# Experts' rows added to their tokens on chip instead of in memory: an encoder block with expert-choice routing, Trainium2

## The chip, the cores and the metric

The kernel runs on one core of a Trainium2 chip. The metric is the device time of one execution in microseconds (us); the figure for the kernel before is the median of three runs. Beside it stands one profiled execution, which the hardware profiler recorded on the chip, and all rows below are from that execution.

## What is computed

A sequence of 512 tokens with 16 learned meta tokens ahead of it (528 rows of 1024 numbers, float32) goes through one layer: attention and a short convolution read one input projection, their outputs are projected back and added to the rows; then comes a mixture of experts, and a last normalisation. Each of 16 experts picks the 66 tokens with the highest affinity:

```python
logits = einsum('ld,de->le', hs, w_router);  aff = softmax(logits)
g, idx = top_k(aff.T, cap)                    # 16 experts x 66 tokens
xg = hs[idx]
a = einsum('ecd,edf->ecf', xg, w_gate);  u = einsum('ecd,edf->ecf', xg, w_up)
y = einsum('ecf,efd->ecd', silu(a) * u, w_down) * g[..., None]
out = zeros((L, D)).at[idx.reshape(-1)].add(y.reshape(-1, D))
h = h + out;   result = rms_norm(h, final_norm_g)[:, 16:, :]
```

Per expert, w_gate and w_up are 1024 x 2048 and w_down is 2048 x 1024: 24 MB of float32, 384 MB for all sixteen, each read once.

## The kernel before

**Up to the routing.** Lines 105 to 905 compute attention, convolution, the projection back (`res_pe`, `res_sum`, lines 794 to 811), the router's affinities and each expert's 66 tokens. The rows after the first half of the layer lie as five tiles of 112 tokens in `h2`. They are written to memory twice: as they are to `acc_d` (lines 845 to 848), and normalised to `hn2_d` (lines 856 to 862). `gather(e)` (line 907) then reads an expert's 66 normalised rows from `hn2_d` with an indirect DMA that POOL issues.

**Weights.** They come as tiles `raw` of 1 MB, one DMA each, into a ring of 22 buffers (`RING = (6, 6, 3, 7)`, line 38). `tasks` (lines 737 to 743) is the order of the tiles: for each expert sixteen of gate and up, and behind every second one a tile of the previous expert's down. `pump(n)` (line 746) issues DMAs on SP's queue until n tiles are under way or waiting; `nextw` (line 947) pumps and hands the next tile to PE. An issue waits until the buffer that it fills has been read.

**The stage of the experts** (lines 998 to 1029) is written in the order in which each engine runs it (`manual_schedule`). For expert e, PE multiplies each gate or up tile by the expert's gathered rows `X` (`prod`, line 951: two column tiles of 64, moving 66 columns, into banks G and U). ACT turns G into silu in `H`, VectorE (DVE) multiplies U into it. Behind every second tile, PE does one `down_piece` of expert e-1 (line 973): `H` is the stationary operand, 22 tokens at a time padded to 32 columns, and a half row of w_down of 512 columns the moving one. Four column tiles run side by side, three groups of tokens one after the other: 12 products, three banks `y`. Two of the four column tiles hold the left half of the outputs and two the right half, each for one half of the contraction.

**down_rows** (line 981) adds the two halves of the contraction and applies the gate, group by group (ACT L986, DVE L987), and POOL adds the 64 half rows of a group to `acc_d` in memory with an indirect DMA that accumulates (L988): three of those for each of the experts 0 to 14.

**The end** (lines 1051 to 1123). The last expert's down is computed transposed (L954 into `bk`), turned (L1076), and added to its tokens by products with a one-hot matrix `oh` (`by_token`, line 1046; L1049). The accumulated rows come back from `acc_d` (L1068), `add` (L1091) joins both, and each row is normalised and stored.

Of the kernel before, what the change touches and what calls it, by code (L numbers as in the profile page):

```python
# [10 lines left out]
F32 = mybir.dt.float32  # L11
# [8 lines left out]
P = 128  # L20
# [17 lines left out]
RING = (6, 6, 3, 7)  # L38
PADS = 10
# [12 lines left out]
def block_kernel(ctx: ExitStack, tc: tile.TileContext, x, meta, mix_g, w_in, conv_w, lq1, lk1, lq2,  # L52
# [708 lines left out]
    xgp = ctx.enter_context(tc.tile_pool(name="xgp", bufs=1, reuse_waits="tile"))  # L761
    rt_p = ctx.enter_context(ExitStack())
    hp = rt_p.enter_context(tc.tile_pool(name="hp", bufs=1, reuse_waits="tile"))
    h2 = hp.tile([P, NT, D], F32, name="h2")
# [7 lines left out]
    jg = hp.tile([P, 3, 2, 22], I32, name="jg")  # L772
    nc.gpsimd.iota(jg, pattern=[[-22, 3], [0, 2], [-1, 22]], base=0, channel_multiplier=1)
    sel = hp.tile([P, 3, 2, 32], F32, name="sel")
    nc.gpsimd.memset(sel, 0.0)
    nc.vector.tensor_scalar(sel[:, :, :, :22], jg, 0.0, None, op0=ALU.is_equal)

    jr = hp.tile([P, 3], I32, name="jr")
    nc.gpsimd.iota(jr[0:32, 0:1], pattern=[[0, 1]], base=0, channel_multiplier=1)
    nc.gpsimd.iota(jr[32:64, 0:1], pattern=[[0, 1]], base=0, channel_multiplier=1)  # L780
    place = hp.tile([P, 3], F32, name="place")
    nc.vector.tensor_scalar(place[:64, 0:1], jr[:64, 0:1], 21.5, None, op0=ALU.is_gt)
    nc.vector.tensor_scalar(place[:64, 1:2], jr[:64, 0:1], 2.0, 2.0 * (L - 22), op0=ALU.mult, op1=ALU.add)
    nc.vector.tensor_tensor(place[:64, 2:3], place[:64, 0:1], place[:64, 1:2], op=ALU.mult)
    nc.vector.tensor_scalar(place[32:64, 2:3], place[32:64, 2:3], 1.0, None, op0=ALU.add)
# [6 lines left out]
    lgt = lg[:TW, :NT * NE].rearrange("p (t e) -> p t e", e=NE)  # L792

    def res_pe(c):

        hT = hT_c[c]
        for t in range(NT):
            nc.tensor.matmul(lgt[:, t], hT[:, T0[t]:T0[t] + TW], wr[:, c], start=c == 0 and t == 0,
                             stop=c == DC - 1 and t == NT - 1)
        pt = tr()  # L800
        for t in range(NT):
            nc.tensor.transpose(pt[:TW, t * P:(t + 1) * P], hT[:, T0[t]:T0[t] + TW], ident)
        nc.scalar.copy(h2[:TW, :, c * P:(c + 1) * P], pt.rearrange("p (t k) -> p t k", k=P)[:TW, :NT])
# [28 lines left out]
    for t in range(NT):  # L832
        for n, a in enumerate(sq_c):
            nc.tensor.matmul(pss[:TW, t:t + 1], a[:, T0[t]:T0[t] + TW], ones[:, 0:1], start=n == 0, stop=n == 1)
    r2 = hp.tile([P, NT], F32, name="r2")
    rsqrt(r2[:TW], pss[:TW, :NT], D)
# [16 lines left out]
    nc.vector.reduce_sum(mx[:TW], af[:TW], axis=AX.X)  # L853
    nc.vector.reciprocal(mx[:TW], mx[:TW])
    nc.vector.tensor_tensor(af[:TW], af[:TW], mx[:TW, :, None].to_broadcast([TW, NT, NE]), op=ALU.mult)
# [85 lines left out]
    for h_ in HS:  # L941
        nc.gpsimd.memset(h_, 0.0)
# [210 lines left out]
```

## Time and profile before

| | us |
|---|---|
| median of three runs (1397.96 to 1399.46) | 1398.5 |
| the profiled execution, own time | 1400.15 |
| its span, from the first to the last instruction | 1398.4 |
| first product of an expert's weights | 350.9 |
| last store issued | 1392.1 |

Busy shares of the span are PE 86%, DVE 22%, ACT 15%, POOL 16%. A matmul in float32 is recorded as two instructions, each with a weight load ahead of it (engine PEld); one in float32r is one. "issue" ahead of an instruction is idle time in which its engine waited for nothing that the profile shows. DMA share is the mean busy share of the core's 16 DMA engines; it reads slightly over 1 where they are never idle.

### The profile page before, as it was taken

To read this page: it belongs to the slowest core of one execution; us is meant where nothing else is said; L and a number is where in the kernel's file an instruction comes from. 1 tells how busy PE (TensorE), PEld (TensorE's weight loads), DVE (VectorE), ACT (ScalarE), POOL (GpSimd) and SP (SyncE) were. 2 spreads that over 40 slices of the span, in tenths; PEclk is the share of its full clock that TensorE was granted. 3 is DMA by queue.
4 is the path that set the end of the run, shared out by engine and by line. 5 is a ranking of instruction groups with operands and counts; after the bars stand their busy time and mean duration, and the time that the engine had idled before them with its cause. 6 is when DMAs were issued, how large, how long until landed. Compare 5 with 4: busy or idle time off the path is not lost.

```text
span 1398.4 us, 46572 instructions
## 1 busy us (share of the span) xinstructions
PE 1201.1 (86%) x22072; PEld 898.7 (64%) x22072; DVE 312.8 (22%) x544; ACT 213.1 (15%) x401; POOL 219.5 (16%) x174
## 2 busy tenths in 40 slices
PE   7897989993789999999999988788888888888884
PEld 6677989993766666666666655555555555555563
DVE  5876777535000100100001000000000100001013
ACT  4455454232000000000000000000000000000002
POOL 2733441332000101101010010101010101000003
PEclk9899999996899999999999999999999999999997
DMA  7311211396999999999999999999999999999994
GB/s 204 91 31 31 61 31 61 125 387 209 392 371 401 396 395 401 389 402 386 396 400 386 397 377 397 388 383 397 384 389 386 394 385 400 389 388 403 403 360 153
DMA packets 147683, 444.67 MB, mean 318 GB/s; under 512 B 14074, under 2 KB 38650, under 8 KB 147492
## 3 DMA queue, kind: packets, MB, share of 16 engines
q1 hardware_dynamic: 140596, 425.69, 79.5%
q0 software_dynamic: 6896, 16.00, 4.6%
q8 instruction: 173, 2.83, 0.8%
q14 instruction: 18, 0.15, 0.0%
HBM read 429.29 MB, written 12.36 MB: 316 GB/s over the span
## 4 chain that ended last, share of the span: by engine, by line
PE 47%; DMA 37%; DVE 6%; issue 5%; ACT 3%; POOL 1%; SPq 1%; POOLq 0%; ACTq 0%; DVEq 0%
DMA raw<-in_w_down 17%; PE y L978 14%; PE G L954 10%; PE U L954 10%; DMA raw<-in_w_gate 9%; DMA raw<-in_w_up 8%; PE pj L274 4%; PE pj L304 3%; DMA acc_rows<-ys,at 1%; PE pj L344 1%; ACT qsw L365 1%; PE sc L430 1%; DMA raw<-in_w_in 1%; ACT p L441 1%; DVE wl L234 1%
## 5 line engine op out<-in xcount | busy, mean ns | idle before, releaser
L978 PE MATMUL y<-raw,H 128*32 128x512 f32 x2880 | 344.8, 601 | 45.9 <-DMA raw<-in_w_down 31.8
L954 PEld LDWEIGHTS U<-X,raw 128*64 128x64 f32 x8192 | 251.3, 138 | 94.6 <-DMA raw<-in_w_up 52.9
L954 PE MATMUL U<-X,raw 128*64 128x66 f32 x8192 | 266.1, 224 | 46.8 <-DMA raw<-in_w_up 27.8
L954 PEld LDWEIGHTS G<-X,raw 128*64 128x64 f32 x8192 | 254.6, 139 | 69.9 <-issue 43.2
L954 PE MATMUL G<-X,raw 128*64 128x66 f32 x8192 | 269.3, 225 | 24.9 <-DMA raw<-in_w_gate 12.7
L978 PEld LDWEIGHTS y<-raw,H 128*32 128x32 f32 x2880 | 85.2, 110 | 208.9 <-issue 160.9
L1026 DVE TENSOR_TENSOR H<-H,U 128x264 f32<-128x264 f32 x64 | 24.6, 426 | 603.0 <-PE U L954 603.0
L988 POOL DMA_INDIRECT acc_rows<-ys,at x45 | 64.1, 1425 | 478.1 <-DVE ys L987 282.0
L1024 ACT ACTIVATE H<-G 128x264 f32<-128x264 f32 x64 | 21.6, 390 | 628.3 <-PE G L954 628.3
L909 POOL DMA_INDIRECT xg<-hn_rows,idxT x16 | 16.1, 1007 | 440.0 <-PE T L966 430.8
L986 ACT ACTIVATE ys<-y,g 64x512 f32<-64x512 f32 x45 | 30.9, 686 | 308.9 <-PE y L978 284.6
L967 DVE TENSOR_TENSOR X<-T,gffn 128x264 f32<-128x264 f32 x32 | 13.8, 433 | 264.6 <-PE T L966 260.4
L274 PE MATMUL pj<-xh,wl 128*128 128x264 f32 x320 | 69.5, 300 | 0.0
L274 PE MATMUL pj<-xl,wh 128*128 128x264 f32 x320 | 68.2, 296 | 0.0
L274 PE MATMUL pj<-xh,wh 128*128 128x264 f32 x320 | 67.4, 293 | 0.0
L274 PEld LDWEIGHTS pj<-xh,wl 128*128 128x128 f32 x320 | 53.1, 202 | 0.1
L274 PEld LDWEIGHTS pj<-xl,wh 128*128 128x128 f32 x320 | 53.0, 201 | 0.0
L274 PEld LDWEIGHTS pj<-xh,wh 128*128 128x128 f32 x320 | 52.4, 198 | 0.0
L987 DVE SCALAR_TENSOR_TENSOR ys<-y,g,ys 64x512 f32<-64x512 f32 x45 | 33.4, 743 | 68.9 <-ACT ys L986 68.9
L234 DVE TENSOR_TENSOR wl<-raw,wh 128x1024 fp32r<-128x1024 f32 x27 | 42.9, 1591 | 2.8 <-ACT wh L232 2.8
L304 PE MATMUL pj<-mx,wh 128*128 128x264 f32 x256 | 41.5, 284 | 0.0
L250 POOL TENSOR_TENSOR raw<-raw,gmix 128x1024 f32<-128x1024 f32 x16 | 33.9, 2134 | 23.6 <-DMA raw<-in_w_in 23.5
(215 smaller groups left out, 925.2 us busy)
## 6 DMA issues: line engine op xcount, KB each, us to landing
raw<-in_w_up SPq DMA_DIRECT2D x128, 1024.0 KB, 19.4
raw<-in_w_gate SPq DMA_DIRECT2D x125, 1024.0 KB, 19.5
raw<-in_w_down SPq DMA_DIRECT2D x125, 1024.0 KB, 19.4
raw<-in_w_in SPq DMA_DIRECT2D x24, 512.0 KB, 5.3
raw<-in_w_out SPq DMA_DIRECT2D x8, 512.0 KB, 3.9
raw<-in_w_gate POOLq DMA_DIRECT2D x3, 1024.0 KB, 9.9
raw<-in_w_down POOLq DMA_DIRECT2D x2, 1024.0 KB, 13.4
raw<-acc_rows SPq DMA_DIRECT2D x4, 512.0 KB, 4.4
```

The lines of the kernel that those rows point to most:

```text
L234: nc.vector.tensor_tensor(lo, src, f32(hi), op=ALU.subtract)
L250: nc.gpsimd.tensor_tensor(self.t, self.t, self.g[:, :, None].to_broadcast([P, DC, P]), op=ALU.mult)
L274: nc.tensor.matmul(o[:, hf * 512:hf * 512 + HALF], a[:, c], b[:, HS[hf]], start=c == 0 and n == 0, stop=c == DC - 1 and n == 2)
L304: nc.tensor.matmul(o[:, hf * 512:hf * 512 + HALF], a[:, k, i * P:(i + 1) * P], b[:, HS[hf]], start=k == 0 and n == 0, stop=k == 3 and n == 2)
L909: nc.gpsimd.indirect_dma_start(out=xg, out_offset=None, in_=hn2_d, in_offset=bass.IndirectOffsetOnAxis(ap=idxT[:CAP, e:e + 1], axis=0))
L954: nc.tensor.matmul(out[64 * q:64 * q + 64], w[:, c0 + 64 * q:c0 + 64 * q + 64], x, start=first, stop=last, skip_group_check=True)
L978: nc.tensor.matmul(y[32 * q:32 * q + 32, g], H[:, 2 * d + ci, g], w[:, ci * 1024 + ob * 512:ci * 1024 + ob * 512 + 512], start=d == 0, sto ...
L986: nc.scalar.activation(ys[:, g], y[64:128, g], AF.Copy, scale=gate)
L987: nc.vector.scalar_tensor_tensor(ys[:, g], y[0:64, g], gate, ys[:, g], op0=ALU.mult, op1=ALU.add)
L988: nc.gpsimd.indirect_dma_start(out=acc_half, out_offset=bass.IndirectOffsetOnAxis(ap=at64[:64, g, e:e + 1], axis=0), in_=ys[:, g], in_offs ...
L1024: nc.scalar.activation(dst, src, AF.Silu)
L1026: nc.vector.tensor_tensor(dst, dst, src, op=ALU.mult)
```

## The change

The sums stay in SBUF: `acc` holds the 512 tokens' rows (four tiles of 128, the meta tokens' rows apart in `hm`, which are only gathered from). `acc_d`, its writes, the 45 accumulating DMAs and the reads at the end are gone. `down_rows` now makes an expert's rows as a pair of float32r tiles (`yh`, the rounded rows, and `yl`, what the rounding left), and POOL a one-hot matrix `oh` of 96 rows by 512 tokens. While the next expert runs, `to_tokens` multiplies `oh` by both, 128 tokens by 512 columns at a time, and DVE adds the result to `acc`: eight times per expert, each ahead of a `down_piece`.

`down_piece` deals its four column tiles differently: three hold the token groups 0 to 31, 32 to 63 and 34 to 65 side by side and read the same half row; the fourth takes the fourth combination of contraction and output half, one group at a time. It stays at 12 products of 32 by 512. Tokens that stand in two groups have gate and index zero in one (`sel`). `H` is dense, without padding. The last part of the ring has 5 buffers for 7, 20 in all.

```diff
-RING = (6, 6, 3, 7)
+RING = (6, 6, 3, 5)
+GR = (0, 32, 34)
...
+    acc = accp.tile([P, 4, D], F32, name="acc")
...
-        nc.scalar.copy(h2[:TW, :, c * P:(c + 1) * P], pt.rearrange("p (t k) -> p t k", k=P)[:TW, :NT])
+        nc.scalar.copy(acc[:, :, c * P:(c + 1) * P], pt[:, :512].rearrange("p (t k) -> p t k", k=P))
+        nc.vector.tensor_copy(hm[:, c * P:(c + 1) * P], pt[:NMETA, 512:640])
...
-    for t in range(NT):
-        f0 = KEEP if t == NT - 1 else 0
-        nc.sync.dma_start(acc_d[T0[t] + f0:T0[t] + TW], h2[f0:TW, t])
-    nc.sync.dma_start(acc_d[L:L + PADS], h2[:PADS, 0])
...
     def down_piece(y, H, d):
         w = nextw()
+        for r in range(3):
+            ob, ci = ((0, 0), (0, 1), (1, 0))[r]
+            o = ci * 1024 + ob * 512
+            for g in range(3):
+                nc.tensor.matmul(y[32 * g:32 * g + 32, ob], H[:, 2 * d + ci, GR[g]:GR[g] + 32], w[:, o:o + 512],
+                                 start=d == 0 and r != 1, stop=d == 7 and r != 0, skip_group_check=True)
+            nc.tensor.matmul(y[96:128, r], H[:, 2 * d + 1, GR[r]:GR[r] + 32], w[:, 1536:2048], start=d == 0, stop=d == 7,
+                             skip_group_check=True)
...
     def down_rows(y, e):
...
+        gate = at96[:96, NE + e:NE + e + 1]
+        nc.scalar.activation(yh[:, a], y[:96, 0], AF.Copy, scale=gate)
+        nc.vector.scalar_tensor_tensor(yl[:, a], y[:96, 0], gate, f32(yh[:, a]), op0=ALU.mult, op1=ALU.subtract)
         for g in range(3):
-            nc.scalar.activation(ys[:, g], y[64:128, g], AF.Copy, scale=gate)
-            nc.vector.scalar_tensor_tensor(ys[:, g], y[0:64, g], gate, ys[:, g], op0=ALU.mult, op1=ALU.add)
-            nc.gpsimd.indirect_dma_start(
-                out=acc_half, out_offset=bass.IndirectOffsetOnAxis(ap=at64[:64, g, e:e + 1], axis=0),
-                in_=ys[:, g], in_offset=None, compute_op=ALU.add)
+            gs = slice(32 * g, 32 * g + 32)
+            nc.scalar.activation(tmp[gs], y[96:128, g], AF.Copy, scale=at96[gs, NE + e:NE + e + 1])
+        nc.vector.scalar_tensor_tensor(tmp, y[:96, 1], gate, tmp, op0=ALU.mult, op1=ALU.add)
+        nc.scalar.copy(yh[:, b], tmp)
+        nc.vector.tensor_tensor(yl[:, b], tmp, f32(yh[:, b]), op=ALU.subtract)
+        nc.gpsimd.tensor_scalar(oh, tok, at96[:96, e:e + 1], None, op0=ALU.is_equal)
+        return oh, yh, yl
+
+    def to_tokens(po, rows, d):
+        oh, yh, yl = rows
+        hf, t = divmod(d, 4)
+        hfs = slice(hf * 512, (hf + 1) * 512)
+        for n, b in enumerate((yh, yl)):
+            nc.tensor.matmul(po, oh[:, t * P:(t + 1) * P], b[:, hfs], start=n == 0, stop=n == 1)
+        nc.vector.tensor_tensor(acc[:, t, hfs], acc[:, t, hfs], po, op=ALU.add)
...
+                    if i % 2 and rows is not None:
+                        to_tokens(banks("T", 1)[:, 0], rows, i // 2)
                     if i % 2 and e:
                         down_piece(y, HS[(e - 1) % 2], i // 2)
...
         if e:
-            down_rows(y, e - 1)
+            rows = down_rows(y, e - 1)
...
+    ps1 = ctx.enter_context(tc.tile_pool(name="ps1", bufs=6, space=PSUM, reuse_waits="tile"))
+    psy = ctx.enter_context(tc.tile_pool(name="psy", bufs=1, space=PSUM))
+    hs = [acc[:, t] for t in range(4)]
...
+        to_tokens(bank(), rows, i)
...
-                    nc.sync.dma_start(t[:, j * D:(j + 1) * D], acc_d[r0:r0 + P])
```

The order of instructions moves in three places. In the rows below, line numbers are those of each kernel's own file (954 became 941, 978 became 968 and 970, 986 became 980 and 984); x31 is a count, and "waits" names the queues and engines that an instruction waits for.

PE, at the first down piece of an expert's turn. G is the bank of the gate products, y that of the previous expert's down, T the bank in which rows are added up per token. Before:

```order
L954 MATMUL G<-X,raw 64x66 [waits DMAHW7_49]
L954 MATMUL G<-X,raw 64x66 x31
L978 MATMUL y<-raw,H_3472 32x512 [waits DMAHW0_49,DVE_49,PE_49]
L978 MATMUL y<-raw,H_3472 32x512 x11
L954 MATMUL G<-X,raw 64x66 [waits DMAHW1_49]
```

The same place in the changed kernel:

```order
L941 MATMUL G<-X,raw 64x66 [waits DMAHW3_49]
L941 MATMUL G<-X,raw 64x66 x31
L998 MATMUL T<-yh,oh 128x512 [waits DVE_49,Activation_49,Pool_49]
L998 MATMUL T<-yl,oh 128x512 [waits DVE_49]
L968 MATMUL y<-raw,H_3464 32x512 [waits DMAHW4_49,DVE_49,PE_49]
L968 MATMUL y<-raw,H_3464 32x512 x2
L970 MATMUL y<-raw,H_3464 32x512
```

Two products over all 128 columns stand ahead of each down piece; the first of an expert waits for the rows of the expert before (ACT, DVE) and for POOL's one-hot matrix, and the down piece still waits for DVE to have read y.

ACT, at the end of an expert's turn, where y is read. Before:

```order
L1024 ACTIVATE H_3472<-G 128x12x22
L986 ACTIVATE ys<-y,g_3447 64x512 [waits DMASW6_49,DMASW5_49,DMASW7_49,DVE_49,PE_49]
L986 ACTIVATE ys<-y,g_3447 64x512 [waits DVE_49] x2
L1024 ACTIVATE H_3471<-G 128x12x22 [waits PE_49]
L1024 ACTIVATE H_3471<-G 128x12x22
```

In the changed kernel:

```order
L1036 ACTIVATE H_3463<-G 128x264
L980 ACTIVATE yh<-y,at_3444 96x512 [waits DVE_49,PE_49]
L984 ACTIVATE tmp<-y,at_3444 32x512 [waits DVE_49]
L984 ACTIVATE tmp<-y,at_3444 32x512 x2
L986 CAST yh<-tmp 96x512 [waits DVE_49]
L1036 ACTIVATE H_3464<-G 128x264 [waits PE_49]
```

Five ACT instructions read or copy where three did, four of them out of y; none waits for a queue of DMAs any more.

PE, where the stage of the experts ends and the last expert's down begins. Before:

```order
L978 MATMUL y<-raw,H_3471 32x512 [waits DMAHW5_49]
L978 MATMUL y<-raw,H_3471 32x512 x11
L954 MATMUL bk<-H_3472,raw 64x66 [waits DMAHW6_49]
L954 MATMUL bk<-H_3472,raw 64x66 x31
L954 MATMUL bk<-H_3472,raw 64x66 [waits DMAHW7_49]
```

In the changed kernel:

```order
L970 MATMUL y<-raw,H_3463 32x512
L941 MATMUL ys_14928<-H_3464,raw 64x66 [waits DMAHW2_49,DVE_49,PE_49]
L941 MATMUL ys_14928<-H_3464,raw 64x66 x31
L998 MATMUL bk<-yh,oh 128x512 [waits Pool_49]
L998 MATMUL bk<-yl,oh 128x512
L941 MATMUL ys_14928<-H_3464,raw 64x66 [waits DMAHW3_49]
```

The first product of the last expert's down now waits for DVE, since its bank is one of y's, and the rows of expert 14 are added between the tiles.

## Rows read from the trace of the kernel before

**Rows 1.** The page's DMA queues: packets, MB, share of 16 engines' span.
```profile
q1 hardware_dynamic: 140596, 425.69, 79.5%
q0 software_dynamic: 6896, 16.00, 4.6%
q8 instruction: 173, 2.83, 0.8%
```
**Rows 2.** Stretches: from:to length, busy time (count) of PE, PEld, DVE, ACT, POOL, clock, DMA, GB/s.
```profile
350.00:408.00 58.00, 43.58 (x1165) 41.99 (x1165) 3.06 (x8) 2.64 (x5) 2.00 (x2) 0.87 1.02 382
408.00:825.20 417.20, 392.27 (x8575) 262.73 (x8573) 32.43 (x63) 23.87 (x49) 34.07 (x26) 1.00 1.03 394
825.20:1290.10 464.90, 393.95 (x8568) 263.18 (x8568) 32.43 (x63) 23.86 (x49) 36.52 (x28) 1.00 1.03 391
```
**Rows 3.** PE's waits from 408 to 825 us: total, times, longest us.
```profile
PE y L978 <- issue: 8.7, 9, 1.8
...
PE y L978 <- PE G L954: 1.9, 4, 0.7
```
**Rows 4.** The same from 825 to 1290 us.
```profile
PE y L978 <- DMA raw<-in_w_down: 29.4, 49, 2.9
```
**Rows 5.** PE's timeline in the first expert's turn: start, length, instruction, count, [idle before].
```profile
368.53 5.37 PE L954 MATMUL U<-X,raw 128*64 128x66 f32 x128 [3.34 <-issue]
...
393.42 3.95 PE L954 MATMUL U<-X,raw 128*64 128x66 f32 x128 [1.76 <-issue]
400.98 1.09 PE L954 MATMUL U<-X,raw 128*64 128x66 f32 x30 [3.62 <-issue]
```
**Rows 6.** PE's timeline in the fourth expert's turn.
```profile
536.65 3.96 PE L954 MATMUL U<-X,raw 128*64 128x66 f32 x128
540.53 2.78 PE L978 MATMUL y<-raw,H 128*32 128x512 f32 x24
543.25 3.96 PE L954 MATMUL U<-X,raw 128*64 128x66 f32 x128
```
**Rows 7.** From 408 to 825 us, turning of X alone: PE, PEld, clock, DMA, GB/s.
```profile
408.00:825.20 417.20, 6.43 (x56) 4.63 (x56) 1.00 1.03 394
```
**Rows 8.** Stretches of 8 us in the eleventh expert's turn, columns as in rows 2.
```profile
956.00:964.00 8.00, 5.86 (x122) 3.61 (x118) 0.74 (x1) 0.06 (x1) 1.42 (x1) 1.00 1.04 391
964.00:972.00 8.00, 6.76 (x153) 4.38 (x150) 0.00 (x0) 0.67 (x2) 1.42 (x1) 1.00 1.03 397
972.00:980.00 8.00, 6.88 (x152) 4.50 (x152) 0.00 (x0) 0.00 (x0) 0.00 (x0) 1.00 1.03 396
...
988.00:996.00 8.00, 7.19 (x158) 4.80 (x157) 0.43 (x1) 0.00 (x0) 0.00 (x0) 1.00 1.02 408
```
**Rows 9.** The timeline at the end of the stage and after it.
```profile
1346.66 2.78 PE L978 MATMUL y<-raw,H 128*32 128x512 f32 x24 [0.46 <-DMA raw<-in_w_down]
...
1349.51 0.69 ACT L986 ACTIVATE ys<-y,g 64x512 f32<-64x512 f32 x1 [16.76 <-PE y L978]
1350.23 0.74 DVE L987 SCALAR_TENSOR_TENSOR ys<-y,g,ys 64x512 f32<-64x512 f32 x1 [3.14 <-ACT ys L986]
...
1359.19 2.09 PE L954 MATMUL bk<-H,raw 128*64 128x66 f32 x64 [0.70 <-DMA raw<-in_w_down]
...
1368.99 1.58 POOL L1063 TENSOR_SCALAR raw<-raw,last 66x512 fp32r<-66x512 int32 x1
...
1372.22 2.11 PE L1049 MATMUL bk<-raw 66*128 66x512 f32 x8
1374.26 0.80 PE L954 MATMUL bk<-H,raw 128*64 128x66 f32 x18
1374.85 0.69 DVE L1093 TENSOR_TENSOR raw<-raw,bk 128x512 f32<-128x512 f32 x1 [10.85 <-DMA raw<-acc_rows]
```
**Rows 10.** POOL's timeline before the stage of the experts.
```profile
344.47 1.20 POOL L909 DMA_INDIRECT xg<-hn_rows,idxT  x1 [9.24 <-DVE vals L905]
...
348.61 0.73 POOL L752 DMA_DIRECT2D raw<-in_w_down  x1
```

More of the change, by code (lines that the diff above doesn't have):

```diff
@@ L769, in block_kernel @@
     nc.vector.tensor_scalar(anti, jq, 0.0, None, op0=ALU.is_equal)
[L772 to L785, printed above, removed]
+    jg = hp.tile([P, 3, 32], I32, name="jg")
+    for k in range(3):
+        nc.gpsimd.iota(jg[:, k], pattern=[[-1, 32]], base=-GR[k], channel_multiplier=1)
+    sel = hp.tile([P, 3, 32], F32, name="sel")
+    nc.vector.tensor_scalar(sel, jg, 0.0, None, op0=ALU.is_equal)
+    nc.vector.memset(sel[:, 2, :64 - GR[2]], 0.0)
     lg = sc()
@@ L797, in res_pe @@
         for t in range(NT):
-            nc.tensor.matmul(lgt[:, t], hT[:, T0[t]:T0[t] + TW], wr[:, c], start=c == 0 and t == 0,
+            nc.tensor.matmul(lgt[:, t], hT[:, U0[t]:U0[t] + P], wr[:, c], start=c == 0 and t == 0,
                              stop=c == DC - 1 and t == NT - 1)
@@ L913, in block_kernel @@
     xg = gather(0)
-    pp64 = pj()
-    for g in range(3):
-        nc.tensor.matmul(pp64[:64, g * 2 * NE:(g + 1) * 2 * NE], sel[:CAP, g].rearrange("p a b -> p (a b)"),
-                         vals2[:CAP].rearrange("p a b -> p (a b)"), start=True, stop=True)
-    at64 = const.tile([P, 3, NE], I32, name="at64")
-    g64 = const.tile([P, 3, NE], F32, name="g64")
+    pp96 = pj()
+    nc.tensor.matmul(pp96[:96, :2 * NE], sel[:CAP].rearrange("p a b -> p (a b)"),
+                     vals2[:CAP].rearrange("p a b -> p (a b)"), start=True, stop=True)
+    at96 = const.tile([P, 2 * NE], F32, name="at96")
     last = const.tile([P, 2], F32, name="last")
-    by_place = pp64[:64, :6 * NE].rearrange("p (g a e) -> p g a e", a=2, e=NE)
-    nc.vector.tensor_scalar(at64[:64], by_place[:, :, 0], 2.0, place[:64, 2:3], op0=ALU.mult, op1=ALU.add)
-    nc.vector.tensor_copy(g64[:64], by_place[:, :, 1])
+    nc.vector.tensor_copy(at96[:96], pp96[:96, :2 * NE])
     nc.vector.tensor_copy(last[:CAP], vals2[:CAP, :, NE - 1])
@@ L939, in block_kernel @@
     NF = DFF // P
-    HS = [wk.tile([P, NF, 3, 32], F32, name=f"H{i}") for i in range(2)]
-    for h_ in HS:
-        nc.gpsimd.memset(h_, 0.0)
+    HS = [wk.tile([P, NF, CAP], F32, name=f"H{i}") for i in range(2)]
+    tok = wk.tile([96, 512], mybir.dt.int16, name="tok")
+    nc.gpsimd.iota(tok, pattern=[[1, 512]], base=NMETA, channel_multiplier=0)
     def banks(tag, n):
@@ L997, in block_kernel @@
     xg = gather(1)
+    rows = None
     for e in range(NE):
```

85 lines of the change are left out of this document (37 added, 48 removed).

## The prediction

> **What bounds the kernel now.** I read four views, from the coarse to the fine.
>
> First the stretches. From 350 to 1290 us the DMA engines' share is 1.02 to 1.03 [rows 2]: they are never idle. 384 MB of weights pass through them, and every other byte in that stage delays weights.
>
> Second, who waits. The last two stretches of rows 2 begin and end where an expert's first down piece starts: that of the second turn at 408.0, of the ninth at 825.2, of the sixteenth at 1290.1. Seven turns lie in each of the last two, and PE runs the same work in both (x8575 and x8568; a turn is 1024 gate and up products, 192 of down and 8 turns of X). Yet the first seven take 417.2 us, 59.6 each, and the second seven 464.9, 66.4 each. In the first seven PE waits for no weights: its waits are "issue" and a little for y [rows 3]. In the second seven it waits for weights, above all those of down [rows 4]. So PE starts behind a ring full of landed tiles, works that lead off until 825, and from there the DMAs set the pace. The end is set by bytes, but PE is only 6.8 us a turn faster.
>
> Third, what sets PE's 59.6. In the first turn, which has no down pieces, a row of 128 products begins at 368.53 behind 3.34 us of "issue", and after four blocks of 128 the next comes at 393.42 behind 1.76 [rows 5]: 24.9 us, 6.2 per block. A lower clock (0.87 in this stretch [rows 2]) is not what holds them: the block at 393.42 runs in 3.95, as blocks do later [rows 6], and still 3.62 of "issue" follow [rows 5]. 128 products are 256 instructions with their weight loads, and the instruction queue moved 173 packets for 44,144 instructions on PE, 255 each [rows 1]. I read this as PE waiting for its next 256 instructions, which come at best every 6.2 us beside saturated DMAs. A turn is 1224 products, 9.56 blocks, 59.3 us at 6.2: nearly the 59.6 found. The work itself is shorter: two tiles take 3.88 and a piece 2.72 [rows 6], 6.6 for three tiles, 52.8 for eight such groups, and turning X takes 0.9 a turn (6.43 in seven [rows 7]).
>
> Here the Trainium skill speaks the other way: its page "Runtime: NRT & Kernel Launch", section "Instruction fetch mechanics", says that instructions are refilled in blocks of 256 and that the cost of crossing a block is mostly hidden. The trace agrees with the block of 256, not with the hiding: it shows 3.34, 1.76 and 3.62 us ahead of blocks [rows 5]. By the rule PE's turn would hold no such slack, and the sum would be the third rival's, 1408.
>
> Fourth, the end. The last down piece of expert 14 starts at 1346.66, having waited for its tile; the last expert's eight tiles keep PE until 1375.06, and from there to the last instruction it is 23.3 us [rows 9].
>
> **The change, part by part.**
>
> *Bytes removed.* 45 accumulating DMAs of 64 rows of 2 KB are 5.9 MB. In three stretches of 8 us with one of them each (POOL's 1.42 us) the engines moved 391, 397 and 396 GB/s, in one without 408 [rows 8]. 40 GB/s missing over 8 us are 0.32 MB, and the three moved 0.39 MB themselves: 0.71 MB fewer weights, 1.75 us per expert. The other bound comes from the queues: POOL's took 4.6% of the span, 64.3 us for 16.0 MB [rows 1]. Five weight tiles, sixteen gathers and the final gain are 10.1 MB of it, 26.4 us at the other queue's 2.61 us per MB (79.5% of the span for 425.69 MB). 37.9 us are left, 2.5 per expert. I take 2.0, nearer the stretches since they compare the same work: 28 us until expert 14's last tile, 30 in all.
>
> *Ring of 20 for 22.* PE starts with a lead that is two tiles shorter: 2 x 1.05 MB at 408 GB/s [rows 8], 5.1 us, is the upper bound. The lower is nothing, since POOL issues the last tiles only at 345 to 349 us [rows 10], and buffers come free soon after 351. I take 5.1, because until 408 PE frees a buffer only every 3.1 us (6.2 per two tiles [rows 5]), slower than a tile lands (2.57).
>
> *The writes of the rows to memory* (2.2 MB ahead of the experts) cost nothing on the path: the first gather is released by DVE's choice of tokens [rows 10], not by a store; with that cover gone it would be their 5.4 us at 408 GB/s. DVE's eight small copies into `hm` I take at nothing; the upper bound is 5.5 us at 0.69 each, the price of a much larger add [rows 9].
>
> *By the DMAs* the last down tile of expert 14 lands at 1346.7 - 28 + 5.1 = 1323.8, and that piece ends 2.7 later, at 1326.5.
>
> *Products added.* Eight products of `by_token`, a pair for each of four times 128 tokens over 66 rows where the new ones have 96, take 2.11 us [rows 9], 0.26 each; 16 per turn are 4.2 us. What hides them is the 6.2 us per block. A block with a piece is 104 gate and up products (3.88 for 128, so 3.15) and 2.72 [rows 6], 5.87 in all, 0.33 under the 6.2; eight of these are 2.6 us. The wait for y adds 0.3 (1.9 us in seven turns [rows 3]), and the turning of X already uses 0.9 [rows 7]. So 2.0 are hidden, 2.2 show: 61.8 per turn. The bounds are 59.6 and 63.8 (all or nothing hidden). The piece itself stays at 12 products of 512 columns on four column tiles; its own 2.72 is the nearest row, and I see no reason for either a gain or a loss.
>
> *The wait for y.* Today ACT and DVE alternate three times, 0.69 and 0.74 [rows 9], about 4.5 us, against two gate tiles of 3.9. Afterwards four ACT reads and one DVE add make 3.5, against 3.9 and the first pair of products. So the down piece does not wait; Behind a pair that waits stand its down piece and all of PE's later tiles, and on SP's queue the next issue, which needs a buffer that they free. DVE's eight adds per turn, 0.69 each, are 5.5 us on an engine that is busy 4.6 of 60 [rows 2]; POOL's one-hot, near 1.58 [rows 9], starts when the previous products have read the old one, a piece earlier. Both stay covered; without cover the pair would wait for them, at most 2 us a turn.
>
> *By PE* the second turn is as today (products start in the third): 408.0 + 59.6 = 467.6; thirteen turns of 61.8 lead to 1271.0; seven eighths of a turn and the piece, 54.1 + 2.7, to 1327.8. So the two bounds nearly meet, and the later, 1327.8, is my end of expert 14's pieces, against 1349.4.
>
> *The end.* The last expert's first product waits for DVE to have read y: 3.5 us (today it starts 1.2 after the piece). Eight tiles then take 2.09 each [rows 9] and a pair of 0.53, 21.0 us; at 6.2 per 128 products, 66 to a tile, 25.6. I take 24, near the upper end as PE has no down pieces there, as in the first turn. The first four `by_token` pairs and a turn are 2.7. Last product: 1327.8 + 3.5 + 24 + 2.7 = 1358.0, against 1375.06, 17.1 earlier. DVE no longer waits 10.85 us for the rows from memory [rows 9], but that ran mostly beside weights; the last pair and add cost 1.2. I take 1.0 less for the rest (bounds: 3 less, 1 more).
>
> Sum: 17.1 + 1.0 = 18.1 under the profiled execution's 1400.15, so 1382.0. The median of the runs is 1.65 lower than that execution: **1380**.
>
> **The rivals.**
>
> *The DMAs alone decide.* If PE's turn is 60.5 or less, the end follows the bytes: with no loss from the ring (5.1), 2.5 for the scatters (7 more) and tiles at 21 in the end (3 less), up to 15 us less, and 1.3 for PE's later end; in the middle of these 1371. For it: PE's waits today are "issue" alone [rows 3], so the blocks hide much. Against it: a ring two tiles shorter must show somewhere in a stage that starts with PE behind.
>
> *Every pair drains PE.* The Trainium skill's page "TensorEngine Tiling (Array Packing)", section "Key Properties", says that changing the tiling mode drains TensorE; a pair over 128 columns between tiles of 64 and of 32 adds one change. The trace shows none for the present change: from the start of 128 products to the piece 3.88 us, and to the next products 2.72 [rows 6], without idle. Priced from rows: 18 products are recorded at 0.80 us [rows 9], 0.26 over their pace of 0.03 each, which is what filling and emptying can cost at most; half of that, eight times a turn, is 1.0. PE's turn is then 62.8, and fourteen turns give back 14 us: 1394, most of the gain gone.
>
> *PE becomes the bound and nothing is hidden.* If the stalls do not absorb the pairs, because they fall in blocks without a piece, PE's turn is 63.8, 2.0 over mine; fourteen of these are 28 us: 1408, slower. It decides from 63.1 us a turn (18.1 / 13.9 over mine), where the whole gain is gone. For it: the stalls that rows 3 count are few and long (nine ahead of y, 8.7 us in seven turns, up to 1.8), so they may be the blocks without a piece. Against it: PE did nothing in 24.9 of 417.2 us [rows 2], 3.6 a turn, and only 1.2 of that is those nine. The rule on instruction fetch above would give this case too.
>
> **How the numbers follow.** My forecast has 0.54, the DMAs alone 0.25, still larger gains 0.04, the drain 0.06, nothing hidden 0.11. A measurement of this kernel can tell 0.2%, 2.8 us, from no change. Of the drain's 0.06 I count half as faster and half as within that, of the last rival 0.02 as within it. Faster by more: 0.54 + 0.25 + 0.04 + 0.03 = 0.86; within it: 0.05; slower: 0.09. The range takes in the bounds: down to 1360 (all of the 15 us above, and the 3 of the end), up to 1400 (a turn of 63.2, most of it unhidden). The rest of the last rival and the largest gains are left out.
>
> **What would show it.** Right: no accumulating DMAs; down pieces of the same length, 2.7; turns of 61 to 62.6 us from the third on, all of one length, with PE idle for "issue" and rarely for weights; expert 14's last piece ends near 1328, the last expert's eighth tile near 1358, some 22 us before the end. Wrong: a turn over 63, idle between a pair and the piece behind it, pieces longer than 2.8, PE waiting for `oh` or `yl`, or DMA shares under 1 before the last expert.

## The result, and the profile after

| | before | after |
|---|---|---|
| median of four runs each, us | 1398.87 (1397.96 to 1399.46) | 1379.45 (1378.40 to 1380.64) |
| the profiled execution, own time | 1400.15 | 1379.79 |
| its span | 1398.4 | 1378.0 |

The ratio is 0.9862, 95% interval 0.9845 to 0.9879: 19.4 us faster. The forecast of 1380 holds, and so does its range. Several of its steps do not, as the experiments show; they cancel. Two executions that were far slower than the others of the same kernel (1486.3 us without scatters, 2854.1 us of the kernel before) are left out of the medians below.

The page of the changed kernel (engines; queues with packets, MB and share; chain; groups of instructions):

```profile
PE 1256.9 (91%) x22308; PEld 927.0 (67%) x22308; DVE 393.1 (29%) x668; ACT 231.2 (17%) x431; POOL 174.9 (13%) x139
...
q1 hardware_dynamic: 139936, 423.49, 80.4%
q0 software_dynamic: 2752, 8.00, 1.9%
q8 instruction: 174, 2.85, 0.8%
...
PE 71%; DMA 12%; DVE 7%; issue 4%; ACT 3%; POOL 2%; SPq 0%; POOLq 0%; DVEq 0%; ACTq 0%
...
L941 PE MATMUL U<-X,raw 128*64 128x66 f32 x8192 | 263.0, 224 | 21.0 <-issue 14.9
...
L999 DVE TENSOR_TENSOR acc<-acc,T 128x512 f32<-128x512 f32 x112 | 76.9, 687 | 599.1 <-PE T L998 599.1
...
L989 POOL TENSOR_SCALAR oh<-tok,at 96x512 fp32r<-96x512 int16 x15 | 23.6, 1573 | 215.9 <-PE T L998 215.8
```

Against [rows 1], POOL's queue has 8.00 MB for 16.00. DVE's 112 adds (0.69 each) and POOL's one-hot tables (1.57) wait for PE.

The stretches of the changed kernel, with the columns of [rows 2], cut at the first down piece of the second, third, fourteenth and sixteenth turn:

```profile
407.00:465.90 58.90, 56.63 (x1227) 37.82 (x1226) 3.90 (x8) 4.43 (x9) 2.54 (x2) 1.00 1.02 396
465.90:1143.70 677.80, 659.92 (x13641) 435.18 (x13640) 108.10 (x187) 51.66 (x100) 28.42 (x22) 1.00 1.02 396
1143.70:1275.40 131.70, 123.09 (x2485) 80.93 (x2487) 20.33 (x35) 9.65 (x19) 4.78 (x4) 0.99 1.02 396
```

The second line is eleven turns, 61.6 us each; two slower ones of 65.9 follow. PE's waits, first in those eleven turns, then from 1143.7 to 1336.1 us (total, times, longest):

```profile
PE G L941 <- issue: 7.5, 9, 1.7
PE U L941 <- issue: 6.4, 9, 1.1
...
PE U L941 <- DMA raw<-in_w_up: 1.3, 1, 1.3
...
PE ys L941 <- DVE tmp L985: 4.5, 1, 4.5
PE U L941 <- DMA raw<-in_w_up: 4.3, 8, 2.0
```

Before, weights set the pace from 825 us on [rows 4]; now only behind 1143, where PE waits 4.3 us for those of up. Around the longest of these waits, 2.0 us, the granted clock is 0.80 (1192 to 1200 us). The timeline of the changed kernel, around a pair of products and then at the end of expert 14 (as [rows 9]):

```profile
1318.49 2.09 PE L941 MATMUL U<-X,raw 128*64 128x66 f32 x64 [0.27 <-DMA raw<-in_w_up]
1320.51 0.50 PE L998 MATMUL T<-yh,oh 96*128 96x512 f32 x1
1320.85 0.40 PE L998 MATMUL T<-yl,oh 96*128 96x512 f32 x1
1321.18 0.63 PE L968 MATMUL y<-raw,H 128*32 128x512 f32 x3
...
1331.60 0.68 ACT L980 ACTIVATE yh<-y,at 96x512 fp32r<-96x512 f32 x1 [18.06 <-PE y L970]
1332.32 0.75 DVE L981 SCALAR_TENSOR_TENSOR yl<-y,at,yh 96x512 fp32r<-96x512 f32 x1 [2.09 <-ACT yh L980]
1333.10 2.07 ACT L984 ACTIVATE tmp<-y,at 32x512 f32<-32x512 f32 x3 [0.81 <-DVE yl L981]
1335.20 0.75 DVE L985 SCALAR_TENSOR_TENSOR tmp<-y,at,tmp 96x512 f32<-96x512 f32 x1 [2.14 <-ACT tmp L984]
...
1336.05 3.27 PE L941 MATMUL ys<-H,raw 128*64 128x66 f32 x64 [4.52 <-DVE tmp L985]
...
1361.04 0.50 PE L998 MATMUL bk<-yh,oh 96*128 96x512 f32 x1
```

A pair takes 0.67 us from its start to the piece behind it, with no idle time around it. The piece that starts at 1321.18 is followed by the next product 2.71 us later, as before (2.72 [rows 6]). Expert 14's last piece ends at 1331.5; PE then stands 4.52 us until DVE has read y, and its next tile takes 3.27 us where others take 2.09. The eighth tile ends at 1361.1, 16.9 us before the end; before it was 23.3.

### The profile page after: what moved, and what is told of

It reads as the page before. It is cut to its first block, busy times and chain, and to the rows that moved or that the text cites. A ratio compares the mean times of both kernels' runs of the same rounds, so it can differ in the third digit from the quotient of the medians.

```text
span 1378.0 us, 47059 instructions
## 1 busy us (share of the span) xinstructions
PE 1256.9 (91%) x22308; PEld 927.0 (67%) x22308; DVE 393.1 (29%) x668; ACT 231.2 (17%) x431; POOL 174.9 (13%) x139
## 4 chain that ended last, share of the span: by engine, by line
PE 71%; DMA 12%; DVE 7%; issue 4%; ACT 3%; POOL 2%; SPq 0%; POOLq 0%; DVEq 0%; ACTq 0%
PE y L968 19%; PE G L941 16%; PE U L941 15%; DMA raw<-in_w_gate 6%; DMA raw<-in_w_up 6%; PE T L998 5%; PE pj L274 4%; PE pj L304 3%; PE ys L941 1%; ACT qsw L365 1%; PE pj L344 1%; PE sc L430 1%; PE T L953 1%; ACT p L441 1%; PE sc L792 1%
## 5 line engine op out<-in xcount | busy, mean ns | idle before, releaser
L968 PE MATMUL y<-raw,H 128*32 128x512 f32 x2160 | 337.1, 596 | 2.0 <-issue 2.0
L970 PE MATMUL y<-raw,H 128*32 128x512 f32 x720 | 332.2, 596 | 0.0
L941 PEld LDWEIGHTS G<-X,raw 128*64 128x64 f32 x8192 | 250.5, 139 | 58.4 <-issue 50.1
L941 PE MATMUL U<-X,raw 128*64 128x66 f32 x8192 | 263.0, 224 | 21.0 <-issue 14.9
L941 PE MATMUL G<-X,raw 128*64 128x66 f32 x8192 | 262.9, 224 | 17.4 <-issue 15.6
L999 DVE TENSOR_TENSOR acc<-acc,T 128x512 f32<-128x512 f32 x112 | 76.9, 687 | 599.1 <-PE T L998 599.1
L968 PEld LDWEIGHTS y<-raw,H 128*32 128x32 f32 x2160 | 79.6, 109 | 190.3 <-issue 175.4
L970 PEld LDWEIGHTS y<-raw,H 128*32 128x32 f32 x720 | 69.0, 109 | 1.3 <-issue 1.0
L980 ACT ACTIVATE yh<-y,at 96x512 fp32r<-96x512 f32 x15 | 10.3, 684 | 281.9 <-PE y L970 281.9
L998 PE MATMUL T<-yh,oh 96*128 96x512 f32 x112 | 55.8, 499 | 1.5 <-issue 1.5
L989 POOL TENSOR_SCALAR oh<-tok,at 96x512 fp32r<-96x512 int16 x15 | 23.6, 1573 | 215.9 <-PE T L998 215.8
L998 PE MATMUL T<-yl,oh 96*128 96x512 f32 x112 | 44.4, 396 | 1.5 <-DVE yl L987 1.5
```

The lines of the kernel that those rows point to most:

```text
L941: nc.tensor.matmul(out[64 * q:64 * q + 64], w[:, c0 + 64 * q:c0 + 64 * q + 64], x, start=first, stop=last, skip_group_check=True)
L968: nc.tensor.matmul(y[32 * g:32 * g + 32, ob], H[:, 2 * d + ci, GR[g]:GR[g] + 32], w[:, o:o + 512], start=d == 0 and r != 1, stop=d == 7 an ...
L970: nc.tensor.matmul(y[96:128, r], H[:, 2 * d + 1, GR[r]:GR[r] + 32], w[:, 1536:2048], start=d == 0, stop=d == 7, skip_group_check=True)
L989: nc.gpsimd.tensor_scalar(oh, tok, at96[:96, e:e + 1], None, op0=ALU.is_equal)
L998: nc.tensor.matmul(po, oh[:, t * P:(t + 1) * P], b[:, hfs], start=n == 0, stop=n == 1)
L999: nc.vector.tensor_tensor(acc[:, t, hfs], acc[:, t, hfs], po, op=ALU.add)
```

## The experiments

Times are medians. The experiments were run in three groups, each beside its own runs of the kernel before, with medians of 1398.73, 1398.39 and 1398.46 us in turn. Times inside an execution are from one profiled execution each. Where expert 14's last piece ends, those of the changed kernel and of four versions of it with the same 20 buffers and products lie between 1331.5 and 1334.4 us, so a difference of 2 or 3 us there is not clear of the spread.

### Where PE's stalls come from

Both kernels, with the weights of all but the first tiles left out:

```diff
     def nextw():
-        pump(NRAW)
-        return queue.pop(0)
+        t = queue.pop(0)
+        used_w.append(t)
+        if len(used_w) > 10:
+            queue.append(t)
+        return t
```

The kernel before:

> The kernel before, but only the first 22 weight tiles are loaded; from then on those on chip are used again in place of loads, so the weights of all later tiles are left out. Scatters, gathers and every instruction of the engines stay. Question: what are TensorE's stalls of 1.4 to 3.6 us after each 256 or so of its instructions (53 to 55 us of work in a turn of 59.6 us)? Theory (they come from what stands beside them, the saturated DMAs, and hide part of any small work that is added): with the DMAs nearly idle the stalls go, a turn falls from 59.6 to 54 to 56 us in all 15 turns, no turn waits for weights, and the time is 1398.9 less (941 - 15 x 55) = 1283 us (1270 to 1300). Rival (the stalls are TensorE's own, or its clock's): a turn stays at 59.6 us, only the waits for weights of the last seven turns go, 1398.9 - (941 - 15 x 59.6) = 1352 us (1345 to 1360).

The changed kernel:

> The changed kernel with the same edit: only the first 20 weight tiles are loaded and are used again, the weights of all later tiles are left out. Theory (the stalls come from the DMAs beside them; the sixteen products of a turn cost their full 16 x 0.26 = 4.2 us where no stall is there to hide part of them): a turn falls from 61.6 to 58 to 60 us, 4.2 us over the same edit of the kernel before, and the time is 1379.5 - (924 - 15 x 59) = 1340 us (1325 to 1355). Rival (stalls stay): a turn stays at 61.6 us and 2.0 us over the kernel before; only the last two turns' waits for weights go, about 1370 us (1365 to 1375). A third reading (the products cost 2.0 us with or without stalls, because they are shorter than 0.26 us or overlap): the difference of the turns of the two edited kernels is 2.0 us, not 4.2.

Measured: 1250.5 us (ratio 0.8942, 0.8927 to 0.8958) and 1315.4 us (0.9403, 0.9381 to 0.9424), both below the first theory's ranges: 18 us of it come from the first turn, which they left out (389.4 at the second turn's first piece for 408.0, and 389.8 for 407.0). The kernel before without loads, its timeline at the first piece of the third and of the sixteenth turn, then its instruction queue between the two:

```profile
444.02 2.78 PE L983 MATMUL y<-raw,H 128*32 128x512 f32 x24 [0.49 <-DVE ys L992]
...
1153.53 2.78 PE L983 MATMUL y<-raw,H 128*32 128x512 f32 x24 [0.48 <-DVE ys L992]
```

```profile
q8 instruction: 125, 2.05, 1.1%
```

Thirteen turns, 54.6 us each, of which 0.5 is a wait for y. The changed kernel without loads, from the fourth turn's first piece to the sixteenth's, and its groups:

```profile
503.45 0.63 PE L973 MATMUL y<-raw,H 128*32 128x512 f32 x3
...
1213.22 0.63 PE L973 MATMUL y<-raw,H 128*32 128x512 f32 x3
```

```profile
L946 PE MATMUL U<-X,raw 128*64 128x66 f32 x8192 | 255.2, 223 | 0.0
...
L946 PE MATMUL G<-X,raw 128*64 128x66 f32 x8192 | 254.9, 224 | 0.0
```

Twelve turns of 59.1 us, with no idle time ahead of 16384 products, where the changed kernel shows 21.0 us for U alone. So the stalls come from the transfers beside PE. Where no stall hides them, the products lengthen the turn by 4.6 us, or 0.29 each (0.31 without the 0.5 us wait for y, which the changed kernel does not have); the reading that they are simply shorter falls.

That PE waits for its instructions there was an inference from the spacing. The packets of the instruction queue in the changed kernel's trace bear it out: in the eleven turns from 465.9 to 1143.7 us PE stands still for more than 0.4 us sixteen times, and each time it starts again 1.3 to 1.6 us after a block has landed.

### The price of the scatters

```diff
-            nc.gpsimd.indirect_dma_start(
-                out=acc_half, out_offset=bass.IndirectOffsetOnAxis(ap=at64[:64, g, e:e + 1], axis=0),
-                in_=ys[:, g], in_offset=None, compute_op=ALU.add)
```

> The kernel before without its three accumulating DMAs per expert, all else as it is; the additions of 15 experts' rows are left out. It prices what the change removes. Theory (the DMAs bound the later turns, each expert's scatters take 2.0 us of them, and the end runs scatter, read back, add): 14 x 2.0 = 28 us earlier at the last weights, a turn from the eighth on of 64.4 us in place of 66.4, and some 3 to 5 us less behind the last product, as the rows read back no longer wait for scatters: 1367 us (1360 to 1373). Rival (the scatters lie beside other transfers that have room): 1394 us (1390 to 1399), with only the end's chain gone.

Measured 1372.4 us (three runs; 0.9814, 0.9793 to 0.9835), near the upper end of the theory's range and far from the rival. Expert 14's last piece ends at 1328.2 for 1349.4: 21.3 us, 1.5 per expert and not 2.0. Behind the eighth tile it is 16.5 us to the end for 23.3, a gain larger than the 3 to 5 expected. The chain that ended last, in the kernel before (start, length, what ran):

```profile
1358.98 7.18 DMA acc_rows<-ys,at
...
1366.89 3.78 DMA acc_rows<-ys,at
...
1372.69 7.61 DMA raw<-acc_rows
1380.32 0.69 DVE raw L1093
```

The end ran along expert 14's scatters, one behind the other, and the read-back that waits for them. Taking out the scatters also made the seven turns from the second on slightly longer, 60.1 us for 59.6 [rows 2], while the DMA engines moved 397 GB/s for 394:

```profile
409.10:829.70 420.60, 394.46 (x8571) 264.13 (x8568) 32.43 (x63) 23.85 (x49) 6.65 (x7) 1.00 1.02 397
```

In the kernel without scatters no such DMA stands in the chain:

```profile
1357.30 1.44 PE bk L1046 x5
...
1358.76 0.70 DVE raw L1090
```

### The price of the products

```diff
-                    if i % 2 and rows is not None:
-                        to_tokens(banks("T", 1)[:, 0], rows, i // 2)
...
-        to_tokens(bank(), rows, i)
```

> The changed kernel without the products that add expert rows to tokens, and without VectorE's additions of them (112 + 8 pairs); the additions of 15 experts' rows are left out. Theory (the sixteen products cost 2.0 us in a turn while TensorE bounds it, and their cost ends where the DMAs bound it): a turn of 59.6 us until weights run short, then turns bound by the DMAs; with the shorter end of the changed kernel 1366 us (1360 to 1372), 8 to 19 us less than the changed kernel. Rival 1 (products hidden whole): 1379 us (1376 to 1382). Rival 2 (nothing of them is hidden): turns of 57.4 us in the first half and the DMAs' bound at the end, also about 1366, so that it is the turn that tells the two apart, not the time.

Measured 1376.7 us (0.9844, 0.9828 to 0.9861): 2.7 less than the changed kernel, inside the range of "hidden whole" and far from the theory's 1366. The first eight turns behind 466.8 took 60.7 us each, without a wait for weights (so "nothing is hidden", 57.4, falls, and the theory's 59.6 is not met either); then weights ran short. That stretch with its instruction queue, and PE's waits from 952 to 1338 us:

```profile
466.80:952.10 485.30, 452.32 (x9792) 302.19 (x9793) 36.65 (x72) 37.54 (x73) 20.77 (x16) 1.00 1.02 396
...
q8 instruction: 77, 1.26, 1.1%
```

```profile
PE U L941 <- DMA raw<-in_w_up: 16.9, 23, 2.4
PE y L968 <- DMA raw<-in_w_down: 16.5, 32, 1.6
```

The changed kernel's 61.6 are only 1.0 more, though the products are 4.6 us of work. Expert 14's last piece ends at 1333.7, no earlier than the changed kernel's 1331.5. Until then the products cost nothing that these traces can show: PE's time without them is waited away for weights three turns sooner than in the changed kernel. What they cost lies in the last eight tiles: from that piece to the end of the eighth tile it is 26.3 us without the pairs and 29.6 with them.

Twice the products:

```diff
-        for n, b in enumerate((yh, yl)):
-            nc.tensor.matmul(po, ..., start=n == 0, stop=n == 1)
+        for n, b in enumerate((yh, yl, yh, yl)):
+            nc.tensor.matmul(po, ..., start=n % 2 == 0, stop=n % 2 == 1)
```

> The changed kernel with each pair of products that adds rows to tokens issued twice into the same bank (the second pair starts the sum again, so the result stays). It asks how much more TensorE's turns could take. What the runs so far show: without transfers beside it sixteen products cost 4.6 us of a turn, beside them 2.0 us, as the stalls shrink from 5.0 to 2.4 us; the DMAs alone want 64 to 66 us of a turn. Theory (the stalls shrink to nothing, and TensorE becomes the bound in every turn): a turn of 59.2 + 4.6 = 63.8 us plus at most 1 us of stalls, 64 to 65 us from the third turn on, expert 14's last piece 14 x 2.8 = 39 us later less the 2 to 4 us for which the changed kernel waited for weights, and 8 x 0.6 = 5 us in the last eight tiles: 1417 us (1405 to 1425). Rival (hidden by half again, or the lead in weights takes it): turns of 62 to 63 us, 1390 us (1385 to 1400).

Measured 1404.0 us (1.0037, 1.0021 to 1.0053), slower than before. The stretch from the fourth turn's first piece to the sixteenth's, and PE's waits in it:

```profile
528.80:1293.10 764.30, 756.08 (x15077) 506.62 (x15080) 117.88 (x204) 56.40 (x109) 30.55 (x24) 1.00 1.02 396
```

```profile
PE U L941 <- issue: 4.0, 7, 1.0
PE G L941 <- issue: 3.3, 5, 1.0
```

Twelve turns of 63.7 us, without waits for weights. The theory's work alone was 63.8, and it put up to 1 us of stalls on top. The total lies just under its range, 13 us under its 1417: the turn is 2.1 us longer than the changed kernel's, not 2.8, and the two turns that waited for weights give back 2.2 each. The rival's turn of 62 to 63 is missed.

### The ring

```diff
-RING = (6, 6, 3, 7)
+RING = (6, 6, 3, 5)
```

> The kernel before with 20 weight buffers in place of 22 (the fourth ring of 5, not 7), nothing else. It prices alone what the change pays for its tables on chip. Theory (the DMAs set when the last weights are there, and two tiles fewer ahead are two tiles of 2.57 us later): 5.1 us slower, 1403.8 us (1402 to 1406), with the last piece of expert 14 ending 5 us later than 1349.4 and turns bound by weights from the sixth or seventh on. Rival (two buffers fewer lie in the lead that TensorE never uses up): no difference, 1398.7 us (1397 to 1400).

Measured 1400.0 us (twelve runs; 1.0009, 1.0001 to 1.0018): 1.6 us, a third of the theory, though not nothing. Its profiled execution, 1395.05, is the fastest of the twelve and does not speak for the median's 1.6.

Inside the change the traces speak for a larger price. What the queues of weights and gathers had moved by 466 us (packets, MB, share), in the kernel before and then in the changed one:

```profile
q1 hardware_dynamic: 49150, 81.38, 50.1%
q0 software_dynamic: 1808, 6.33, 3.8%
```

```profile
q1 hardware_dynamic: 48575, 79.37, 48.6%
q0 software_dynamic: 1264, 4.23, 2.7%
```

The changed kernel is 4.1 MB behind. 2.2 of these are the writes of the rows, which the change takes out; 1.9 MB are left, 4.8 us at the 396 GB/s of the stage, near the 5.1 forecast. Part of it may come from a later start, since the first product of an expert's weights comes at 353.5 us for 350.9. The kernels without scatters and without products, 1328.2 and 1333.7 at expert 14's end, put the smaller ring and the rest of the change together at 5.5 us. What part of this is the buffers alone stays open.

### The wait ahead of the last expert

```diff
-    ps1 = ctx.enter_context(tc.tile_pool(name="ps1", bufs=6, space=PSUM, reuse_waits="tile"))
     psy = ctx.enter_context(tc.tile_pool(name="psy", bufs=1, space=PSUM))
+    ps1 = ctx.enter_context(tc.tile_pool(name="ps1", bufs=6, space=PSUM, reuse_waits="tile"))
```

> The changed kernel with the two pools of the last expert's stage opened in the other order, so that the banks of its first product are two that the gate and transposes had, not two that expert 14's rows are still read from. The wait of 4.52 us ahead of the first of the eight tiles then falls on the first pair that adds rows to tokens, one tile of 2.1 us later. Theory (nothing but TensorE's order stands there, the weights of these tiles have landed): 2.1 to 3.3 us faster than the changed kernel, 1376.7 us (1376 to 1377.5). Rival (the DMAs set the eight tiles' pace): 1379.4 us, the time gained is waited for weights behind it.

Measured 1379.9 us (0.9864, 0.9850 to 0.9878): no gain, but not for the rival's reason either. The timeline shows the old wait in its old place:

```profile
1338.59 0.71 PE L941 MATMUL ys<-H,raw 128*64 128x66 f32 x8 [4.52 <-DVE tmp L985]
```

So the choice of banks alone was not it. With the pair moved as well:

```diff
-        to_tokens(bank(), rows, i)
+        for k in ((), (0, 1))[i] if i < 2 else (i,):
+            to_tokens(bank(), rows, k)
```

> As the run with the pools in the other order, and the first pair that adds expert 14's rows to tokens is issued behind the second of the eight tiles, together with the second pair. TensorE then has two tiles, 4.2 us, to do while VectorE and ScalarE make the rows (4.5 us). Theory: the whole wait of 4.5 us and the part of the first tile at half clock (3.27 against 2.09 us) go: 5 to 6 us faster than the changed kernel, 1374 us (1373 to 1375.5), as far as weights have landed. Rival (weights set the pace): TensorE waits for the second to fourth tile, no more than 2 to 3 us gained, 1377 us.

Measured 1380.3 us (0.9868, 0.9854 to 0.9883): nothing either, for the same 4.52 us stand in its trace. What was left was the pool: `psy` is opened without the argument that the pools beside it have.

```diff
-    psy = ctx.enter_context(tc.tile_pool(name="psy", bufs=1, space=PSUM))
+    psy = ctx.enter_context(tc.tile_pool(name="psy", bufs=1, space=PSUM, reuse_waits="tile"))
```

> As the run with the two pools in the other order, which left the wait of 4.52 us as it was; now the pool of the first product's two banks waits for those that had its own place, and not for all of the old pool (one argument where it is opened). Theory (the wait was for expert 14's rows through the whole old pool): the first tile starts within 1 us of expert 14's last piece, the first pair waits for the rows instead, some 3 us, and 1.2 to 2.3 us are gained against the changed kernel: 1377.5 us (1376.5 to 1378.5). Rival (weights that land only then): the first tile still starts 2 us or more later, no gain.

Measured 1376.3 us (0.9835, 0.9814 to 0.9856; runs 1373.3 to 1377.5, all below those of the changed kernel), 3.2 better than the changed kernel and more than expected. Its timeline:

```profile
1333.88 2.09 PE L941 MATMUL ys<-H,raw 128*64 128x66 f32 x64
...
1334.76 0.75 DVE L981 SCALAR_TENSOR_TENSOR yl<-y,at,yh 96x512 fp32r<-96x512 f32 x1 [2.12 <-ACT yh L980]
...
1335.90 0.50 PE L998 MATMUL bk<-yh,oh 96*128 96x512 f32 x1
...
1336.56 1.95 PEld L941 LDWEIGHTS ys<-H,raw 128*64 128x64 f32 x64 [0.36 <-DMA raw<-in_w_down]
```

The first tile runs at once, in 2.09 us and not 3.27. The first pair does not wait for the rows, as I had thought it would: it reads their first half, which is made by 1335.5. Then weights are due, a wait of 0.36 us. So little was left for the next run to find:

> Both: the pool waits by place, and the first pair is issued behind the second tile. Theory: two tiles (4.2 us) lie in the 5 to 6 us in which the rows are made, the last tile ends 4.5 us earlier than in the changed kernel, 1375 us (1374 to 1376.5); the weights are no bound, since the last of them landed near 1350 us in the changed kernel, 11 us ahead of the last product on them. Rival (weights set the pace of these tiles): 1377.5 us, no better than the run with the pair in its place.

Measured 1375.5 us (0.9833, 0.9813 to 0.9853), the same within the spread (1373.9 to 1377.4). The time lies inside the theory's range, 4.0 us under the changed kernel, but 3.2 of it are the pool's alone; the second tile ahead of the pair adds nothing clear of the spread, because the 3 us that it meant to cover were not there.

One buffer more, on the kernel with the pair later and then on the one with both edits:

```diff
-RING = (6, 6, 3, 5)
+RING = (6, 6, 3, 6)
...
-        yh = wk.tile([96, D], FR, name="yh", tag="yh")
+        yh = wk.tile([96, D], BF, name="yh", tag="yh")
...
-        tmp = wk.tile([96, 512], F32, name="tmp", tag="tmp")
+        tmp = H.rearrange("p f n -> p (f n)")[:96, :512]
```

> As the run with the first pair later, and one weight buffer more (21): room for it comes from keeping the expert's rows and the one-hot table as 16-bit floats in two parts (high and rest), and from a scratch row in the hidden tile that is no longer read. The products are as many. Theory (each buffer is one tile of 2.57 us in the lead at the end): 2.6 us faster again, 1371.5 us (1370 to 1373). Rival 1 (the first rival of the run with 20 buffers: the lead is not what decides): the same as without the buffer. Rival 2 (16-bit products are shorter and that alone changes the time): turns of the first half fall below 61.6 us by up to 2 us, with the same end, since the weights set it.

> The same with one more weight buffer, as the run with 21 buffers made room for it. That run and the kernel before with 20 buffers put a buffer at 0.8 to 1.4 us, where the prediction had 2.57. Theory: 1.4 us under the run with both edits, 1373.6 us (1372.5 to 1375). Rival (with the wait gone the end of the weights is what is left, and a buffer counts in full): 2.6 us, 1372.4 us. A third: nothing, as the eight tiles are TensorE's.

Measured 1378.8 us (0.9857, 0.9843 to 0.9872), 1.4 under the run without the buffer, with runs that overlap (1377.0 to 1379.6, and 1378.5 to 1382.1), and 1373.1 us (0.9817, 0.9798 to 0.9837; 1372.2 to 1374.1), 2.4 under its counterpart, inside the theory's range, with the rival's 1372.4 not excluded. The 2.6 of the first of the two theories is not reached. The turns did not shorten by 2 us with the 16-bit rows (61.5 us in the eleven turns from the third on with the pair later and 21 buffers, 61.6 in the changed kernel), so the rival on their length falls; that part of the 1.4 and 2.4 comes from the shorter pairs of the last tiles was not separated. The last kernel is the best of all: 25.4 us under the kernel before and 6.4 under the changed one, with no run in common with it.

## Why the prediction was right, and which steps were not

**PE's turn: right in its ground and its total, not in its parts.** 61.8 was forecast, 61.6 measured in eleven turns. Its ground, that PE waits for blocks of 256 instructions beside busy DMAs, is borne out by the runs without loads and by where the stalls end. The instruction queue (packets, MB, share) of the changed kernel in those eleven turns, then of the kernel before from 408.0 to 825.2, then of the doubled products from 528.8 to 1293.1:

```profile
q8 instruction: 107, 1.75, 1.1%
```

```profile
q8 instruction: 67, 1.10, 1.1%
```

```profile
q8 instruction: 118, 1.93, 1.0%
```

That is 9.73, 9.57 and 9.83 blocks a turn, 6.33, 6.23 and 6.48 us apart. A turn is close to the longer of two times: its work (54.6 before, 59.1 after, by the runs without loads), and its blocks at 6.2 to 6.3 us. Before, the blocks are longer (59.6), after still (61.6); with twice the products the work is, 59.1 + 4.6 = 63.7, as measured.

The step "2.0 are hidden, 2.2 show" does not hold. Taking out the products shortens the turn by 1.0 us only (61.62 to 60.66), so 1.0 show and 3.6 are hidden, of 4.6; their 32 instructions are an eighth of a block, 0.8 us at 6.3 by estimate. The other 1.1 us over the 59.6 come with the rest of the change, for which the forecast put nothing into the turn. 0.5 of it appears in the kernel before as soon as its scatters go (60.1 us); the cause of the rest stays open. That the turn came out at its forecast is luck in the parts.

The Trainium skill's page "Runtime: NRT & Kernel Launch", section "Instruction fetch mechanics", calls the cost of crossing a block mostly hidden: the changed kernel without loads agrees (0.0 us idle ahead of gate and up products), the changed kernel itself does not (14.9 us of "issue" ahead of U alone).

**Bytes removed: mis-sized.** "I take 2.0" per expert; taking the scatters out gave 21.3 us until expert 14's end, 1.5 each, below both bounds (1.75 from the stretches, 2.5 from the queues). This is the step behind the others' errors: with it the DMAs' end is not 1326.5 but 1333.7 (the run without products) or 1331.5 (the changed kernel itself), behind PE's 1327.8. With 21.3 in place of 28 the forecast's own sum for the DMAs, with its 5.1 for the ring, gives 1333.2. So "the later, 1327.8, is my end" failed by 3.7 us: two turns of 65.9 us, in which weights run short, stand where it had 61.8, and the 2.2 us a turn for which it charged the products are not on the path.

**Ring of 20 for 22: size open.** 5.1 taken; 1.6 in the kernel before, 1.4 and 2.4 for one buffer in versions of the changed one, and 4.8, by the bytes moved until 466 us, for two buffers and a later start in the changed one itself.

**The wait ahead of the last expert: right in kind.** 4.52 us, where four reads and an add were put at 3.5; they take 1331.60 to 1335.95, 4.35, because ACT's second read waits 0.81 for DVE's `yl`, which the sum left out. The clock was not foreseen: behind these 4.52 us without work, from 1336.05 to 1339.3, PE was granted 0.60 on average, between its levels of 1.2 and 2.4 GHz, and the tile took 1.2 us longer. The eight tiles and what lies between took 25.1 for 24 + 2.7.

**The rest of the end: failed.** "1.0 less (bounds: 3 less, 1 more)"; it is 6.4 less, 16.9 for 23.3. "That ran mostly beside weights" was wrong: the last scatters and the read-back were the chain itself, and the kernel without scatters has 16.5.

The sum of the errors: 3.7 + 1.0 - 1.6 - 5.4 = -2.3, from 1382.0 to the profiled 1379.8. The number was right by cancelling.

**Costs put at nothing** held, but for the turn's 1.1 us above: the second turn's first piece comes at 407.0 for 408.0 with the copies into `hm`, although the first product of an expert's weights comes 2.6 us later; in the eleven turns PE waits neither for `oh` nor for `yl`, and later once for `yl`, 1.5 us. That wait, and a DMA share of 0.99 from 360 to 408 us, are two of the forecast's signs of being wrong, both small. Pieces are still 2.7.

**The rivals.** "The DMAs alone decide" has the mechanism of the result until expert 14's end, though its condition (a turn of 60.5 or less) is not met, and not its time: its gain of up to 15 us took 2.5 for a scatter and nothing for the ring. "Every pair drains PE" did not come, neither its turn of 62.8 nor its 1394, and no idle time stands around the pairs; but a pair takes 0.66 us (median of 112) where 0.53 was summed, so a drain of up to 0.13 a pair, hidden in the stage, is not excluded. "Nothing is hidden" did not occur, but doubled products show that it was priced well: a turn of 63.7 is past its point of 63.1, and that kernel is slower than before, 1404.0 for its 1408.

## What to carry to other kernels

Where two bounds nearly meet, try each one alone, by taking out the transfers or the added work: the products with one-hot tables were free in the stage here because the weights came later anyway, and a forecast that charges them is right only by luck. A turn that grows with a change need not have grown by what was added: of 2.0 us here only 1.0 went when the products were taken out. When accumulating scatters feed a read-back, look for them in the chain at the end, not only among the bytes. A wait at a change of pools may be for the old pool and not for the data: here one argument, on top of the pools' order, gave 3.2 us, where the order and a moved pair alone gave nothing. The argument without the order was not tried.

## What was not expected of the hardware

Next to idle DMAs PE fetched a block of instructions every 5.7 us (125 in 709.5 us) without a wait, and next to busy ones every 6.2 to 6.3 us with waits of up to 2 us: transfers of data slow an engine that waits for no data. And 45 accumulating DMAs on POOL's queue, 5.9 MB, cost 26.3 us in all, less than foreseen in the stage (1.5 us per expert) and more at the end (23.3 us behind the eighth tile, 16.5 without them).
